# Keys and values written to DRAM once, with the loads making the doubled and shifted copies

## The chip, the cores and the metric

The kernel runs on one core of a Trainium2 chip. The metric is device time in microseconds of one execution, the median of several runs; lower is better. A core has TensorE (PE: matrix products and transposes), VectorE (DVE), ScalarE (ACT), GpSimd (POOL) and SyncE (SP, which here issues DMA transfers), each with its own list of instructions that it works through in order. Transfers are issued from SP's list and from POOL's.

## The reference, cut to what matters

One layer on a sequence of 2048 tokens with 1024 channels, all float32. Sixteen query heads share four key and value heads of 64 channels; attention reaches back over 128 positions.

```python
h = rms_norm(x, norm_g)
u = h @ w_in
v_c, b_c, c_c, z_c, q, k, v, z_a, gate_logits = split(u)
y_c = b_c * causal_depthwise_conv(c_c * v_c, conv_w) * silu(z_c)
y_a = y_c @ w_conv_out
q = rms_norm(q per head, q_norm_g); k = rms_norm(k per head, k_norm_g)
o = sliding_window_attention(q, k, v, sinks) * silu(z_a)   # banded blocks of 128
y_b = o @ w_attn_out
g_a, g_b = split(sigmoid(gate_logits + gate_b))
return x + (g_a * y_a + g_b * y_b) @ w_out
```

## The kernel before

The sequence is worked through in two tiles of T = 1024 tokens, each as two halves of H = 512. Products run at full float32 accuracy by splitting every operand into a high part and a low part (`split`): high by high, high by low and low by high. Most projections (`sunit`) form seven such products in place of eight by a Strassen-like scheme; the first tile's keys and values come from a plain unit (`cunit`).

The order of all work is written out by hand. `run` advances a counter, the tick, once for each piece of a TensorE unit, some 2.7 to 3.5 us; `put(n, f)` places a step `f` at tick `n`, and `ahead_loads` issues weight loads two units ahead, from SP. A tick therefore fixes the order of instructions in each engine's list, and the semaphores between engines fix the rest.

Temporary tiles of 2 KB a partition come from one pool of 19 buffers (`big`, through `slot`). Which buffer a tile gets is decided when the program is built, by the builder's reckoning of which falls free first; the first write to a tile then waits for the last use of the tile that had the buffer before.

Per tile of tokens the order is: keys, values, four units of queries, then the convolution's units (`cv`, `b`), gates (`ga`, `gb`), the two gated branches (`za`, `z`), and the branch outputs (`ya`, `yb`). The last stage, `o`, is for the whole sequence.

Keys, queries and values go to DRAM scratch tensors and come back in the arrangement that the attention wants:

- `fin_q` (L605) writes a normalised query's high and low part to `q2d`, four writes for each 512 tokens of a unit, from POOL.
- `fin_k` (`back`, L672) writes a key unit's high and low part to `kd`, one write for each of two heads and each part, from POOL. A head's 64 channels are written twice, to partitions 0 to 63 and 64 to 127.
- `fin_v` (L699) writes values, token on the partitions, to `vd[block, partition, kind, head, high and low]`. There are four kinds for each block: the block itself (kind 1), the block shifted by 64 tokens (kind 0), and each of its and its predecessor's halves doubled over both halves of the partitions (kinds 2 and 3). Each pair of blocks takes seven writes, from POOL. `zero_prev` fills the part of the first block that has no predecessor.

`attention` places, for each of 8 blocks of 128 tokens and 4 key heads of a tile, seven steps: `att_load` at tick n - 4 (from SP: queries L714, keys L719 or L721 and L723, values L725), `att_scores` at n (L738: eight products of a query tile as stationary operand with 192 key columns as moving operand), `att_exp`, `att_norm`, `att_turn` (transposes, then four selections on POOL, L792), `att_values` at n + 7 (L809) and `att_out` (from SP, L822). The values tile `v2` is the stationary operand of `att_values`.

## Time and profile before

| | |
|---|---|
| runs | 2031.86, 2033.07, 2033.2 us; median 2033.07 |
| the profiled execution: its own time | 2032.55 us |
| its span, first to last instruction | 2030.8 us |
| granted TensorE clock, mean | 0.999 |
| busy: TensorE, DVE, ACT, POOL | 2002.3, 1385.3, 936.9, 429.2 us |
| DMA | 329.15 MB, mean 162 GB/s |
| writes of values and keys, from POOL | 112 and 32, median 0.61 us to issue |
| landing of those writes, median | 3.6 to 4.0 and 5.4 to 6.0 us |
| loads of queries, keys and values, from SP | 64, 68 and 64; landing 3.6 to 4.4 us |

The rows are read from the profile of one execution. A busy row adds up the time of an engine's instructions, without those that issue transfers; the times of those come from the groups by line. "Waited for" names the event that ended an engine's idle time, with the total, the number of times and the longest. A row of the timeline gives the start, the duration, the engine, the line, the operation, output and input, and in square brackets the idle time just before it with what ended it. Clock 1.00 is full speed.

### The profile page before, as it was taken

Reading aid. Unit: us, or ns where it says so; the run is one execution under the profiler, and the core shown is the slowest. Engines: PE = TensorE matmul, PEld = TensorE weight load, DVE = VectorE, ACT = ScalarE, POOL = GpSimd, SP = SyncE. Lnnn points to the kernel's source line nnn. Section 1 sums busy time; section 2 is a strip of 40 time slices with the busy share of each in tenths; the row PEclk is TensorE's granted clock in tenths of the full one; section 3 lists DMA queues with packets and bytes.
Section 4 is the critical chain, followed back from the end, with each engine's and each line's share of the span. In section 5 each row is a group of like instructions: output and inputs, shape, how many; then the busy total and the mean of one; then the engine's idle time right before and its main releaser. Section 6 shows DMA issues by size and latency. Waiting matters only on the chain.

```text
span 2030.8 us, 27523 instructions
## 1 busy us (share of the span) xinstructions
PE 2002.3 (99%) x9488; PEld 1664.3 (82%) x9488; DVE 1385.3 (68%) x2360; ACT 936.9 (46%) x1847; POOL 429.2 (21%) x597
## 2 busy tenths in 40 slices
PE   8999999999999999999999999999999999999999
PEld 6787888888888887888878888888888887888887
DVE  6877787787675555348768887787776656356654
ACT  6554455456664333244545544455665334212321
POOL 1873222222321000000277222222332000100000
PEclk9999999999999999999999999999999999999999
DMA  6794424445555534664498434445555443765553
GB/s 177 223 241 137 131 83 122 133 131 173 156 173 164 176 110 148 230 221 154 126 255 215 128 100 138 128 122 168 162 177 173 148 146 129 249 214 167 174 171 109
DMA packets 339594, 329.15 MB, mean 162 GB/s; under 512 B 21804, under 2 KB 260448, under 8 KB 339456
## 3 DMA queue, kind: packets, MB, share of 16 engines
q1 hardware_dynamic: 321984, 276.37, 43.9%
q0 software_dynamic: 17456, 51.04, 9.2%
q8 instruction: 75, 1.23, 0.2%
q14 instruction: 63, 0.52, 0.1%
q10 hardware_dynamic: 16, 0.00, 0.0%
HBM read 217.61 MB, written 109.71 MB: 161 GB/s over the span
## 4 chain that ended last, share of the span: by engine, by line
PE 71%; DVE 4%; ACT 3%; issue 3%; DMA 1%; POOL 1%; SPq 0%; POOLq 0%; DVEq 0%; ACTq 0%
PE Y L364 21%; PE yb L938 9%; PE ya L938 8%; PE Vcv L364 2%; PE Xcv L364 2%; PE Xza L364 2%; PE Vz L364 2%; PE Vo L364 2%; PE Xo L364 2%; PE Xz L364 2%; PE Vza L364 2%; PE s L738 2%; PE Xgb L364 2%; PE po L809 1%; PE Xga L364 1%
## 5 line engine op out<-in xcount | busy, mean ns | idle before, releaser
L792 POOL TENSOR_SCALAR_AFFINE_SELECT xh<-xh 64x512 fp32r<-64x512 f32 x64 | 69.4, 1085 | 644.7 <-DVE xl L784 477.6
L763 ACT ACTIVATE p<-s,st,rq 128x128 f32<-128x128 f32 x256 | 113.5, 453 | 0.6
L699 POOL DMA_DIRECT2D vd<-v x112 | 69.4, 626 | 197.3 <-DVE v L207 186.4
L210 DVE TENSOR_TENSOR o<-po,o 64x256 f32<-64x256 f32 x128 | 53.7, 420 | 67.4 <-ACT o L820 61.2
L971 DVE SCALAR_TENSOR_TENSOR tha<-tha,ya 128x512 f32<-128x512 f32 x32 | 22.0, 687 | 100.8 <-PE ya L938 93.9
L820 ACT COPY o<-po 64x256 f32<-64x256 f32 x128 | 47.0, 367 | 83.6 <-DVE o L210 82.1
L938 PE MATMUL ya<-opa,wya_0h 128*128 128x512 f32 x256 | 79.5, 391 | 2.4 <-ACT opa L206 1.9
L364 PE MATMUL Xcv<-oph,wcv_ah 128*128 128x512 f32 x256 | 80.1, 394 | 0.0
L938 PE MATMUL yb<-opb,wyb_0h 128*128 128x512 f32 x256 | 79.4, 391 | 0.0
L938 PE MATMUL yb<-opb,wyb_1h 128*128 128x512 f32 x256 | 79.4, 391 | 0.0
L938 PE MATMUL ya<-opa,wya_1h 128*128 128x512 f32 x256 | 78.8, 389 | 0.0
L738 PEld LDWEIGHTS s<-k,q 128*128 128x128 f32 x512 | 65.6, 191 | 9.0 <-ACT p L763 5.4
L206 ACT CAST opb<-ocr 128x512 fp32r<-128x512 f32 x32 | 19.9, 621 | 111.5 <-DMA ocr<-ocd 109.8
L784 DVE TENSOR_TENSOR xl<-pt,xh 128x512 fp32r<-128x512 f32 x64 | 44.1, 690 | 39.7 <-ACT yp L783 33.9
L738 PE MATMUL s<-k,q 128*128 128x192 f32 (+2 forms) x512 | 67.2, 274 | 2.9 <-ACT p L763 2.7
L991 DVE SCALAR_TENSOR_TENSOR thb<-thb,yb 128x512 f32<-128x512 f32 x32 | 21.9, 686 | 55.2 <-PE yb L938 53.5
L938 PEld LDWEIGHTS ya<-opa,wya_0h 128*128 128x128 f32 x256 | 48.0, 188 | 13.6 <-ACT opa L206 2.8
L858 DVE SCALAR_TENSOR_TENSOR y<-u,cols,y 128x512 f32<-128x512 f32 x64 | 50.1, 784 | 10.6 <-ACT y L851 8.6
L1025 POOL DMA_DIRECT2D wo<-in_w_out x16 | 8.7, 544 | 226.1 <-DVE opb L207 209.7
L938 PEld LDWEIGHTS ya<-opa,wya_1h 128*128 128x128 f32 x256 | 48.1, 188 | 10.0
L792 POOL TENSOR_SCALAR_AFFINE_SELECT yp<-xl 64x512 fp32r<-64x512 f32 x64 | 55.3, 864 | 3.1
L938 PEld LDWEIGHTS yb<-opb,wyb_1h 128*128 128x128 f32 x256 | 47.6, 188 | 9.6
(583 smaller groups left out, 6246.3 us busy)
## 6 DMA issues: line engine op xcount, KB each, us to landing
wcv_raw<-in_w_in SPq DMA_DIRECT2D x64, 256.0 KB, 4.6
q<-q2d SPq DMA_DIRECT2D x64, 256.0 KB, 3.7
v<-vd SPq DMA_DIRECT2D x64, 256.0 KB, 4.4
gd<-th SPq DMA_DIRECT2D x64, 256.0 KB, 2.2
k<-kd SPq DMA_DIRECT2D x56, 256.0 KB, 4.4
vd<-v POOLq DMA_DIRECT2D x96, 128.0 KB, 3.6
wq_raw<-in_w_in SPq DMA_DIRECT2D x32, 256.0 KB, 4.3
q2d<-q_h POOLq DMA_DIRECT2D x64, 128.0 KB, 4.9
```

Source lines behind the costliest of these rows:

```text
L210: return (eng or nc.vector).tensor_tensor(out=o, in0=a, in1=b, op=ALU.add)
L364: nc.tensor.matmul(ps, lhsT=w[:, j, :], rhs=b[:, m, :], start=start and j == 0 and i == 0, stop=j == KP - 1 and i == 2, skip_group_check=n ...
L699: nc.gpsimd.dma_start(to.rearrange("b p h d -> p b h d"), v[half].bitcast(F32).rearrange("p b e l d -> p b e (l d)"))
L738: nc.tensor.matmul(sp[:, h, c, skip : 3 * HD], lhsT=q2[:, h, c, :], rhs=k2[:, l, h * HD + skip : h * HD + 3 * HD], start=l == 0, stop=l == 1)
L763: nc.scalar.activation(out=p[:, i, :], in_=sg[:, i, HD : 3 * HD], func=AF.Exp, bias=st[:, 1, i : i + 1], scale=rv[:, i // 2, i % 2 : i % 2 ...
L784: nc.vector.tensor_tensor(out=xl, in0=pt, in1=xh.bitcast(F32), op=ALU.subtract)
L792: nc.gpsimd.affine_select(out=d4, in_=s4, pattern=[[0, 2 * G], [-sg, HD]], compare_op=ALU.is_gt if prev else ALU.is_ge, fill=0.0, base=0, ...
L820: nc.scalar.copy(ov, pov[oth, :, :, e, :])
L858: nc.vector.scalar_tensor_tensor(out=y, in0=u[:, h * H + i : h * H + i + H], scalar=tap(i, k), in1=y, op0=ALU.mult, op1=ALU.add)
L938: nc.tensor.matmul(ps, lhsT=w[:, j, cs], rhs=o[:, m, :], start=p == 0 and j == 0 and i == 0, stop=p == 1 and j == KP - 1 and i == 2)
L971: nc.vector.scalar_tensor_tensor(out=m, in0=m, scalar=1.0, in1=ps, op0=ALU.add, op1=ALU.mult)
L991: nc.vector.scalar_tensor_tensor(out=m, in0=m, scalar=1.0, in1=ps, op0=ALU.add, op1=ALU.mult)
```

## The change

Keys and values are written once, and the loads make the copies.

- `kd[t]` becomes `[head, channel, half block of 64 tokens, high or low, 64]`. `back` issues two writes for each call, one for each part, with both heads in one write; a partition's 512 tokens go out as eight runs of 64. The load reads the 64 channels twice, into both halves of the partitions (`twice`), and the tile `k2` is now ordered by half block and then part, so that the moving operand of the scores is three pieces of 64 columns.
- `vd` becomes `[token + 128, head, high and low]`. One call of `fin_v` issues two writes in place of fourteen, one for each pair of blocks. `att_load` issues four value loads in place of one: the two full arrangements (kinds 0 and 1), each of 128 tokens, and the doubled halves, once into each half of the partitions.
- `zero_prev` is one write in place of three.

The order of TensorE, DVE and ACT instructions is the same in both programs. SP has 192 more transfers to issue, POOL 114 fewer.

```diff
-    kd = [dram.tile([NKV, P, 2, T], F32, name=f"kd{t}") for t in range(NT)]
-    vd = dram.tile([S // P + 1, P, 4, NKV, P], F32, name="vd")
+    kd = [dram.tile([NKV, HD, 2 * NB, 2, HD], F32, name=f"kd{t}") for t in range(NT)]
+    vd = dram.tile([S + P, NKV, P], F32, name="vd")
...
     def zero_prev():
-        nc.gpsimd.dma_start(vd[0, LH, 0], zv[LH])
-        for n in (2, 3):
-            nc.gpsimd.dma_start(vd[0, :, n], zv)
+        nc.gpsimd.dma_start(vd[0:P].rearrange("p h d -> p (h d)"), zf)
...
             split(hi, lo, pt)
-            for e in range(2):
-                for l, src in enumerate((hi, lo)):
-                    nc.gpsimd.dma_start(
-                        kd[t][2 * i + e, :, l, hs(q)].rearrange("(o d) t -> d o t", d=HD),
-                        src[HALVES[e]].bitcast(F32).unsqueeze(1).to_broadcast([HD, 2, H]))
+            for l, src in enumerate((hi, lo)):
+                nc.gpsimd.dma_start(
+                    kd[t][2 * i : 2 * i + 2, :, q * 2 * HB : (q + 1) * 2 * HB, l].rearrange(
+                        "o d b x -> (o d) b x"),
+                    src.bitcast(F32).rearrange("p (b x) -> p b x", x=HD))
...
-                    b0 = t * NB + q * HB + 2 * bp
-                    ALL = slice(0, P)
-                    for kind, off, dst, half in (
-                            (1, 0, ALL, ALL), (0, 0, UH, LH), (0, 1, LH, UH),
-                            (2, 1, LH, LH), (2, 1, UH, LH), (3, 1, LH, UH), (3, 1, UH, UH)):
-                        to = vd[b0 + off : b0 + off + 2, dst, kind, 2 * i : 2 * i + 2, :]
-                        nc.gpsimd.dma_start(
-                            to.rearrange("b p h d -> p b h d"), v[half].bitcast(F32).rearrange("p b e l d -> p b e (l d)"))
+                    r0 = t * T + q * H + (2 * bp + 1) * P
+                    nc.gpsimd.dma_start(
+                        vd[r0 : r0 + 2 * P, 2 * i : 2 * i + 2].rearrange("(b p) h d -> p b h d", p=P),
+                        v.bitcast(F32).rearrange("p b e l d -> p b e (l d)"))
...
+    def twice(ap):
+        return ap.unsqueeze(0).to_broadcast([2] + list(ap.shape))
...
-        k2 = slot([P, 2, 2 * P], F32R, f"k2_{nm}")
+        k2 = slot([P, 4, 2, HD], F32R, f"k2_{nm}")
...
         if b > 0:
-            nc.sync.dma_start(k2.bitcast(F32), kd[t][j, :, :, (b - 1) * P : (b + 1) * P])
+            nc.sync.dma_start(
+                k2.bitcast(F32).rearrange("p b l x -> p (b l x)"),
+                twice(kd[t][j, :, 2 * b - 2 : 2 * b + 2].rearrange("d b l x -> d (b l x)")))
...
-        nc.sync.dma_start(v2.bitcast(F32), vd[gb, :, :, j, :])
+        r0 = gb * P
+        for i in range(2):
+            nc.sync.dma_start(v2[:, i].bitcast(F32), vd[r0 + (1 + i) * HD : r0 + (3 + i) * HD, j])
+        for half in HALVES:
+            nc.sync.dma_start(
+                v2[half, 2:4].bitcast(F32), vd[r0 : r0 + P, j].rearrange("(n k) d -> k n d", n=2))
...
-                        rhs=k2[:, l, h * HD + skip : h * HD + 3 * HD], start=l == 0, stop=l == 1)
+                        rhs=k2[:, h + skip // HD : h + 3, l, :], start=l == 0, stop=l == 1)
```

More of the change, by code (lines that the diff above doesn't have):

```diff
@@ L151, in block_kernel @@
     hbias = consts.tile([P, 2 * KC], F32, name="hbias")
-    zv = zf.rearrange("p (h d) -> p h d", d=P)
     def zero_prev():
-        nc.gpsimd.dma_start(vd[0, LH, 0], zv[LH])
-        for n in (2, 3):
-            nc.gpsimd.dma_start(vd[0, :, n], zv)
+        nc.gpsimd.dma_start(vd[0:P].rearrange("p h d -> p (h d)"), zf)
     def prep_gain():
@@ L716, in att_load, with keys @@
             q2d[t][j][:, 2 * b : 2 * b + 2].rearrange("p h c e x -> p (h c e x)"))
-        k2 = slot([P, 2, 2 * P], F32R, f"k2_{nm}")
+        k2 = slot([P, 4, 2, HD], F32R, f"k2_{nm}")
+        def keys(n, t, b):
+            nc.sync.dma_start(
+                k2[:, n : n + 2].bitcast(F32).rearrange("p b l x -> p (b l x)"),
+                twice(kd[t][j, :, 2 * b : 2 * b + 2].rearrange("d b l x -> d (b l x)")))
         if b > 0:
-            nc.sync.dma_start(k2.bitcast(F32), kd[t][j, :, :, (b - 1) * P : (b + 1) * P])
+            nc.sync.dma_start(
+                k2.bitcast(F32).rearrange("p b l x -> p (b l x)"),
+                twice(kd[t][j, :, 2 * b - 2 : 2 * b + 2].rearrange("d b l x -> d (b l x)")))
         else:
-            nc.sync.dma_start(k2[:, :, P:].bitcast(F32), kd[t][j, :, :, 0:P])
+            keys(2, t, 0)
             if gb > 0:
-                nc.sync.dma_start(k2[:, :, :P].bitcast(F32), kd[t - 1][j, :, :, T - P : T])
+                keys(0, t - 1, NB - 1)
         v2 = slot([P, 4, P], F32R, f"v2_{nm}")
-        nc.sync.dma_start(v2.bitcast(F32), vd[gb, :, :, j, :])
+        r0 = gb * P
+        for i in range(2):
+            nc.sync.dma_start(v2[:, i].bitcast(F32), vd[r0 + (1 + i) * HD : r0 + (3 + i) * HD, j])
+        for half in HALVES:
+            nc.sync.dma_start(
+                v2[half, 2:4].bitcast(F32), vd[r0 : r0 + P, j].rearrange("(n k) d -> k n d", n=2))
         return q2, k2, v2
```

## The prediction

> **What bounds the kernel.** I read the page's busy row and slices first, then the waits of TensorE, then the timeline round the longest of them.

> ```profile
> span 2030.8 us, 27523 instructions
> PE 2002.3 (99%) x9488; PEld 1664.3 (82%) x9488; DVE 1385.3 (68%) x2360; ACT 936.9 (46%) x1847; POOL 429.2 (21%) x597
> ...
> POOL 1873222222321000000277222222332000100000
> ```

> TensorE works through one fixed list and is idle for 28.5 us in all. The change leaves that list as it is, so it can win only from those 28.5 us (and any stretch at a lower clock), and lose by adding idle time. POOL, off the path on average, is at 7 to 8 tenths in slices 2, 3, 21 and 22: there it issues the writes of v, k and q for each tile of 1024 tokens. TensorE's own waits, longest first (total, times, longest):

> ```profile
> PE s L738 <- ACT p L763: 2.7, 4, 1.2
> PE Y L1098 <- POOL zero L129: 2.6, 1, 2.6
> PE Y L364 <- DVE Vq L210: 2.2, 1, 2.2
> PE pt L779 <- DVE p L216: 2.2, 2, 1.8
> PE ya L938 <- ACT opa L206: 1.9, 2, 1.0
> PE ptq L572 <- DVE qss L581: 1.6, 1, 1.6
> ```

> No wait is on a load. Two of these places hang on what the change touches.

> **Second tile, q units (1015 to 1068 us).** Start, duration, instruction, and in brackets the idle time before it:

> ```profile
> 1016.69 0.72 ACT L600 ACTIVATE q_h<-q_t,gqk 128x512 fp32r<-128x512 f32 x1
> 1055.59 0.71 POOL L605 DMA_DIRECT2D q2d<-q_h  x1 [0.81 <-DMA vd<-v]
> 1056.83 0.75 DVE L601 SCALAR_TENSOR_TENSOR q_l<-q_t,gqk,q_h 128x512 fp32r<-128x512 f32 x1 [7.67 <-DMA kd<-k_l]
> 1053.21 0.73 PE L364 MATMUL Y<-oph,wq_sh 128*128 128x512 f32 x2 [0.73 <-ACT Y L382]
> 1061.17 0.73 PE L364 MATMUL Y<-oph,wq_th 128*128 128x512 f32 x2 [2.20 <-DVE Vq L210]
> ```

> The first q half is ready at 1017.4 and its write is issued at 1055.6: POOL's queue is 38 us behind with v and k. Tiles not yet written out keep their buffers of the pool of 19, so DVE stands 7.7 us for one, and TensorE 0.73 + 2.20, and 0.3 more at 1067.7.

> **First attention block (166 to 194 us).**

> ```profile
> 167.34 0.59 ACT L434 COPY q_t<-Y 128x512 f32<-128x512 f32 x1 [3.52 <-PE s L738]
> 167.39 0.75 DVE L601 SCALAR_TENSOR_TENSOR q_l<-q_t,gqk,q_h 128x512 fp32r<-128x512 f32 x1 [4.42 <-PE s L738]
> 168.89 1.09 PE L572 MATMUL ptq<-ident,q_t 128*128 128x128 f32 x4 [1.59 <-DVE qss L581]
> 186.17 0.69 DVE L784 TENSOR_TENSOR xl<-pt,xh 128x512 fp32r<-128x512 f32 x1 [2.00 <-issue]
> 194.07 0.50 PE L364 MATMUL Vcv<-oph,wcv_sl 128*128 128x512 f32 x1 [1.34 <-DVE wcv_sl L270]
> ```

> In the built program, which gives each tile's address and no time, `q_t` and `q_l` of the last q unit lie in the buffers of block 0's keys and queries, and `xl` of block 0 in that of block 1's queries. So ACT and DVE wait for scores that TensorE reaches by its list, and TensorE then waits for them.

> **The change, part by part.**

> *POOL's issues.* Per tile, 56 writes of v and 16 of k become 8 and 8. Before: 48 at 0.61, 8 at 0.72 (the full-width v rows), 16 at 0.61: 44.8 us. After: v 8 at 0.72; a key write is 128 partitions of eight 256-byte runs, and its nearest row is the q write's 0.69 for 64 such partitions; ends 0.61 and 1.4, I take 0.85. Sum 12.6, so 32 us less per tile. POOL also idles for landings there (0.4 to 1.7 us each time), and 56 fewer transfers shorten that too. The last k_l is ready at 1011.9; POOL then issues it by about 1013, before the first q half. The 3.2 us of TensorE go: **-3.2** (ends 0 and -3.7, by which its products start later there than their pace). In tile 0 the same backlog costs TensorE no row of its own; I take nothing.

> *Buffers.* The planner hands out buffers by its own reckoning of when they fall free. With fewer writes, 926 of the 1065 tiles change place. In the built changed program `q_t` and `q_l` follow q tiles that are long done, and `xl` follows one too. Holding each tile's first write in the trace against the last use of its new predecessor (POOL's writes moved up as above), one wait is new: block 2's keys for block 0's `p`, 175.8 to 182.5, on SP. Behind it queue block 2's v and the next weights; scores come at 202.4, and v itself waited until 191.3 before. So 1.6 at 168.9 goes, and at 194.07, where `xl` can start 2 us sooner, 1.3: **-2.9** (ends 0 and -3.3).

> *The clock.* Two stretches, with busy times of PE, PEld, DVE, ACT and POOL, then the granted clock, DMA share and GB/s:

> ```profile
> 165.40:168.80 3.40, 1.90 (x13) 1.59 (x11) 1.41 (x3) 1.43 (x3) 0.25 (x1) 1.00 0.18 48
> 168.80:172.30 3.50, 3.41 (x10) 2.91 (x11) 3.50 (x5) 2.27 (x4) 3.50 (x6) 0.51 0.64 119
> ```

> After the stretch with TensorE busy for 1.90 of 3.40 us comes one at half clock, costing half of 3.4. Without the gap: **-1.7** (ends 0 and -1.7). [...]

> *SP.* A block's v load becomes four issues of 128 runs each; the nearest rows are 0.32 to 0.43 for 128 runs, so 1.5 against 0.55; the key load has half as many pieces. That is +1.0 a block, 64 us over both tiles, in front of SP's next entries: stores, weight loads, the next q. Weight loads are read 17 us or more after issue. After a v load SP mostly stands 1 to 15 us for a store's data, which hides it. Pushing every later issue back until the next such stand moves 8 of 64 q loads, by at most 1.3 us, each with 10 us or more in hand. **0** (ends 0 and +21, first rival). The bytes written fall by 8.4 MB a tile; DMA's share is 0.5 in these stages, so nothing.

> *Key layout.* The scores' moving rows become three pieces of 64 columns.

> ```profile
> 166.29 1.00 PE L738 MATMUL s<-k,q 128*128 128x64 f32 x8
> 401.23 1.03 PE L738 MATMUL s<-k,q 128*128 128x192 f32 x8
> ```

> Eight products of 64 and 128 columns take as long as eight of 192: the weight load sets the pace, and a short break hides under it. No row has such a layout. **0** (ends 0 and +17, second rival).

> Sum: -3.2 - 2.9 - 1.7 = -7.8. The profiled execution is 2032.55 (span 2030.8 and 1.75 round it), 0.5 under the median of 2033.07; from the median, **2025.3 us**.

> **Rivals.** A measurement of this kernel tells about 0.2% (4.1 us) from no change.

> - *SP late (slower).* Place: q and k loads with the least lead. At 1355.49 a q load goes out for scores at 1362.8; the key load follows 0.5 later and lands in 4.4 at the median, so 2.4 are left; 15 of 64 blocks have leads under 9.5, 3.6 spare on average. It decides from 3 us of delay; at 5 us they lose 15 x 1.4 = 21: 2046. For it: a q issue held 1.85 at 1361.92 by earlier transfers. Against: these 15 follow a store's wait, not a v load. 0.06.
> - *Broken key rows (slower).* 512 columns pass in 0.227 us, so 192 in 0.085; the pace of 0.111 leaves 26 ns, 13 a break. At 30 a break, 34 x 504 = 17: 2042. For it: no row. Against: the pair above. 0.05.
> - *Late key writes.* The runs of a key write shrink from 2 KB to 256 bytes and could land late. Rows: q writes of 256-byte runs land in 4.7 to 4.9 us, k writes of 2-KB runs in 5.4 to 6.0, so no penalty is seen. [...] With eight in flight, 16 writes pace POOL as before only from 44.8 x 8 / 16 = 22 us each; then the 3.2 stay: 2028.5. 0.05.
> - *One place only is mended.* DVE, busy 75.6 of the 105 us from 995 to 1100, stays late by itself: 2028.5; or the first block's stall returns by another buffer: 2029.9. 0.15, half each.
> - *Nothing moves*: the writes were hidden anyway and other buffers bind: 2033. 0.07.

> The forecast has 0.62.

> **The numbers.** Faster by over 0.2% (under 2029.0): 0.62 + 0.05 + 0.07 = 0.74. Same: 0.08 + 0.07 = 0.15. Slower 0.11. Range: down to 2022.5, as the ends of the two waits give 0.9 more and the runs before spread by 1.3; up to 2030.5, past both halves of the partial case. That leaves out 0.07 + 0.11 and little else.

> **What would show it.** Right: POOL's first q write of tile 1 within some us of its data; no `Y <- Vq` or `ptq <- qss` wait; no half clock at 168.8; scores at 0.11 a product; v in four issues near 0.38. Wrong: TensorE waits on `k` or `v` loads, scores over 0.12 a product, key writes landing after 20 us, or fresh waits of ACT or DVE on buffers.

## The result, and the profile after

The changed kernel takes 2043.29 us (median of 6 runs, 2039.83 to 2045.7), the kernel before 2032.22 (6 runs beside it): a ratio of 1.0053, 95% interval 1.0042 to 1.0065, so 11 us slower where 8 us faster was forecast.

The head of the profile after, and TensorE's waits in the whole span (total, times, longest):

```profile
span 2041.3 us, 27651 instructions
PE 2007.0 (98%) x9488; PEld 1665.9 (82%) x9488; DVE 1385.4 (68%) x2360; ACT 936.7 (46%) x1847; POOL 363.5 (18%) x483
...
POOL 1353222222220000000253222222232000100000
```

```profile
PE s L750 <- DMA k<-kd: 11.4, 12, 1.9
PE Y L1110 <- POOL zero L131: 2.6, 1, 2.6
PE s L750 <- DMA wb_raw<-in_w_in: 2.1, 1, 2.1
```

POOL's slices 2, 3, 21 and 22 fell from 7 and 8 tenths to 5 or less, as forecast. (POOL's busy row does count the instructions that issue its transfers, other than the note under the first table says: its 597 became 483, which are the 114 writes fewer.) Two of the waits shown before, `Y <- Vq` (2.2) and `ptq <- qss` (1.6), are gone. In their place the scores wait for key loads, 11.4 us in twelve waits; the wait put down to `wb_raw` is one more of them, at a block whose key load had gone out 9.4 us earlier. In the profile before, TensorE waited for no load.

POOL's queue at the second tile's q units, the first q half's high part and the first write of it:

```profile
1017.02 0.72 ACT L598 ACTIVATE q_h<-q_t,gqk 128x512 fp32r<-128x512 f32 x1
1019.49 0.70 POOL L603 DMA_DIRECT2D q2d<-q_h  x1 [0.21 <-issue]
```

It is 2 us behind, not 38. Both programs give TensorE the same 9488 products in the same order, so the starts can be subtracted pair by pair. The changed kernel gains 5.0 us between 150 and 200 us and 4.1 at the second tile's q units, the two places of the forecast, and loses 19.8 elsewhere, nearly all of it in waits right ahead of scores and in three stretches at half clock; the sum is +10.7. Such a loss, with the key load's issue (SP), the scores that wait for it (PE), and two windows of 3.41 us, the one that holds the wait and the next (columns as in the windows of the prediction):

```profile
579.97 0.53 SPq L721 DMA_DIRECT2D k<-kd  x1
589.64 1.11 PE L750 MATMUL s<-k,q 128*128 128x192 f32 x8 [1.93 <-DMA k<-kd]
```

```profile
587.90:591.31 3.41, 1.67 (x11) 1.57 (x12) 2.55 (x4) 1.07 (x2) 0.99 (x1) 1.00 0.44 118
591.31:594.72 3.41, 3.41 (x10) 2.64 (x9) 1.73 (x5) 0.00 (x0) 0.00 (x0) 0.50 0.74 211
```

The keys went out 7.7 us before TensorE was ready for them and came 1.9 too late; then TensorE ran a window at half clock. Where scores wait, they start 8.3 to 9.7 us after the key load's issue. In the kernel before, scores started as little as 6.8 after the issue without waiting for keys, and key loads landed in 4.4 at the median (number, KB of each, median us to landing):

```profile
k<-kd SPq DMA_DIRECT2D x56, 256.0 KB, 4.4
```

### The profile page after: what moved, and what is told of

Same layout as the page of the kernel before. It is cut to its first block, busy times and chain, and to the rows that moved or that the text cites. A ratio compares the mean times of both kernels' runs of the same rounds, so it can differ in the third digit from the quotient of the medians.

```text
span 2041.3 us, 27651 instructions
## 1 busy us (share of the span) xinstructions
PE 2007.0 (98%) x9488; PEld 1665.9 (82%) x9488; DVE 1385.4 (68%) x2360; ACT 936.7 (46%) x1847; POOL 363.5 (18%) x483
## 4 chain that ended last, share of the span: by engine, by line
PE 70%; DVE 9%; issue 7%; DMA 5%; ACT 3%; POOL 2%; SPq 1%; POOLq 0%; DVEq 0%; ACTq 0%
PE Y L362 21%; PE yb L950 9%; PE ya L950 8%; DMA k<-kd 4%; PE Xcv L362 3%; PE Vcv L362 3%; PE Xza L362 2%; PE Vz L362 2%; PE Vo L362 2%; PE Xo L362 2%; PE Xz L362 2%; PE Vza L362 2%; PE Vq L362 2%; PE Xq L362 2%; PE s L750 2%
## 5 line engine op out<-in xcount | busy, mean ns | idle before, releaser
L750 PE MATMUL s<-k,q 128*128 128x192 f32 (+2 forms) x512 | 69.0, 277 | 15.4 <-DMA k<-kd 11.4
L794 ACT CAST xh<-pt 128x512 fp32r<-128x512 f32 x64 | 37.4, 585 | 40.3 <-PE pt L791 39.5
L362 PEld LDWEIGHTS Xcv<-oph,wcv_ah 128*128 128x128 f32 x256 | 48.1, 194 | 9.4
L950 PEld LDWEIGHTS yb<-opb,wyb_0h 128*128 128x128 f32 x256 | 47.6, 188 | 9.6
```

Source lines behind the costliest of these rows:

```text
L362: nc.tensor.matmul(ps, lhsT=w[:, j, :], rhs=b[:, m, :], start=start and j == 0 and i == 0, stop=j == KP - 1 and i == 2, skip_group_check=n ...
L750: nc.tensor.matmul(sp[:, h, c, skip : 3 * HD], lhsT=q2[:, h, c, :], rhs=k2[:, h + skip // HD : h + 3, l, :], start=l == 0, stop=l == 1)
L794: nc.scalar.copy(xh, pt)
L950: nc.tensor.matmul(ps, lhsT=w[:, j, cs], rhs=o[:, m, :], start=p == 0 and j == 0 and i == 0, stop=p == 1 and j == KP - 1 and i == 2)
```

## The theories and the experiments

Theory 1: the doubled load reads a source whose outermost dimension is 2 (`twice` puts the copies in front of the 64 channels), so it is spread over 2 of the 16 DMA engines. For it, before any run: the packet counts. Each of the kernel before's 1052 SP transfers left 16 small completion packets in queue 1 (4 bytes, 16832 in all); of the changed kernel's 1244 transfers, 952 such packets are missing (18952 are there), which is 14 for each of the 68 key loads and leaves 2. A key load is 128 runs of 2 KB at 84 ns each (the median of those packets): by these, an estimate, 64 x 84 ns = 5.4 us on two engines and 0.7 on sixteen. That an outermost dimension of 2 gives two engines is so far the theory; the packets alone show the 2. Rivals: SP issues too much (theory 2), or reading rows twice, or the new layout in DRAM, is slow in itself (theory 3).

### Two key loads, one for each half of the partitions

```diff
-                twice(kd[t][j, :, 2 * b - 2 : 2 * b + 2]...)
+            for half in HALVES:
+                nc.sync.dma_start(k2[half]..., kd[t][j, :, 2 * b - 2 : 2 * b + 2]...)
```

Expected: 

> The changed kernel with each block's key load made as two loads, one for each half of the partitions, 64 rows each; one issue more a block. Theory 1 (the doubled load, whose source has an outermost dimension of 2, runs on 2 of the 16 DMA engines and lands about 9 us after its issue, where 4.4 did before; TensorE then waits for keys): the loads are spread over 16 engines again and land in 4 to 5 us, TensorE waits on no key load, the time is 2022 to 2026. Theory 2 (SP issues too much and is late): with 0.3 to 0.5 us more of issue in a block the waits on key loads stay or grow, 2043 to 2060. Theory 3 (the same DRAM rows read twice, or the new key layout in DRAM, are slow in themselves): as changed, 2040 to 2046.

Measured: 2025.05 us against 2031.36 of the kernel before, 0.9965 (0.9953 to 0.9978). No wait on a key load is left, and the load lands in less than half the time (KB of each, median us to landing):

```profile
k<-kd SPq DMA_DIRECT2D x112, 128.0 KB, 3.9
```

Theory 1 holds and the others fall: one more issue a block, the same rows read twice and the same layout, and yet 18 us less than the changed kernel.

### The other way round: the kernel before with a source of 2 x 64 rows

```diff
-  nc.sync.dma_start(k2.bitcast(F32), kd[t][j, :, :, (b - 1) * P : (b + 1) * P])
+  nc.sync.dma_start(k2.bitcast(F32), twice(kd[t][j, 0:HD, :, (b - 1) * P : (b + 1) * P]))
```

Expected: 

> The kernel before, its DRAM layout and issues kept; only the key load reads its first 64 rows twice (the second 64 hold the same numbers), so that its source has an outermost dimension of 2. Theory 1: key loads land in 8.5 to 9.5 us, TensorE gets waits on key loads that the kernel before lacks, and the time rises by 12 to 25 us, to 2044 to 2057. Theory 2: the issues are the same, so no change, 2030 to 2034. Theory 3 in its part on layout: no change; in its part on rows read twice: slower as in theory 1.

Measured: 2075.9 us, 1.0217 (1.0203 to 1.0231). The fault alone costs 44 us in the kernel before; the direction is theory 1's, the size is well beyond its 12 to 25. The group of the scores' products (busy, mean ns, and behind the second bar the idle time ahead of them), here and then in the kernel before:

```profile
L742 PE MATMUL s<-k,q 128*128 128x192 f32 (+2 forms) x512 | 70.6, 281 | 33.6 <-DMA k<-kd 27.4
```

```profile
L738 PE MATMUL s<-k,q 128*128 128x192 f32 (+2 forms) x512 | 67.2, 274 | 2.9 <-ACT p L763 2.7
```

That is 31 us more of idle time, and ten windows at half clock in place of one, 9 x 1.7 = 15; a few us come back elsewhere. In its waits the scores start 9.3 to 11.1 us after the key load's first issue, and 13.7 at one block (the second tile's first); the median is 9.9, and 9.0 in the changed kernel. About half of that difference is, by an estimate from the packets' medians (46 ns for 1 KB, 84 for 2 KB), the load's 256 runs of 1 KB, 128 x 46 ns = 5.9 us on an engine in place of 5.4. The issues did not stay the same in one respect: the value load behind the key load held SP for 3.0 us at the median, in the kernel before for 0.55. Why, and how much of the 44 us it makes, is open. The estimate had counted neither this nor the half clock.

The number of packets in queue 1 (then MB, and the share of 16 engines), here and in the kernel before, differs by the same 952:

```profile
q1 hardware_dynamic: 321032, 276.36, 43.4%
```

```profile
q1 hardware_dynamic: 321984, 276.37, 43.9%
```

### As many engines as copies: the dose

The changed kernel, its key load reading 8 rows sixteen times, or 32 rows four times, in place of 64 rows twice; bytes, issues and buffers stay, and wrong keys reach the scores.

```diff
-        return ap.unsqueeze(0).to_broadcast([2] + list(ap.shape))
+        return ap[0 : P // 16].unsqueeze(0).to_broadcast([16, P // 16] + list(ap.shape[1:]))
```

Expected of sixteen: 

> The changed kernel, its key load reading the first 8 of the 64 rows sixteen times (outermost dimension 16) in place of 64 rows twice: same bytes, same issues, same buffers; wrong keys reach the scores, only its time is read. Theory 1: 16 engines, landing 4 to 5 us, 2022 to 2026. Theories 2 and 3 (issues; rows read more than once): 2040 to 2050, waits on key loads as in the changed kernel.

Expected of four: 

> The changed kernel, its key load reading 32 rows four times (outermost dimension 4) in place of 64 rows twice; wrong keys reach the scores, only its time is read. Theory 1: 4 engines, each with 32 runs of 2 KB at 84 ns, 2.7 us in place of 5.4 on two and 0.7 on sixteen; landing 6 to 7 us after the issue, with 7.2 as the least lead: few or no waits, 2022 to 2028. If the rows read again are slow, or a fixed cost of a doubled source is what delays it: 2038 to 2046.

Measured: sixteen 2024.31 us, 0.9960 (0.9948 to 0.9973); four 2026.62, 0.9977 (0.9968 to 0.9986). Queue 1 (packets, MB, share of 16 engines) with two, four and sixteen copies:

```profile
q1 hardware_dynamic: 315400, 276.38, 43.9%
```

```profile
q1 hardware_dynamic: 315536, 276.38, 44.4%
```

```profile
q1 hardware_dynamic: 316352, 276.38, 45.1%
```

Against sixteen copies, two lack 952 packets, 68 x 14, and four lack 816, 68 x 12: read as one for each engine, the completion packets count 2, 4 and 16 engines. With two loads a block there are 317440 packets, 68 x 16 more than with sixteen copies: all sixteen engines for each load. With sixteen the load lands in 4.7 us at the median and no score waits for it; the block shown above got its keys without a wait 7.6 us after the issue. With four, TensorE stands idle ahead of three scores for 1.4 us in all, 0.7 at most. Reading rows again cost nothing by itself: 2024.31 us with 8 rows read sixteen times, 2025.05 with 64 rows in each of two loads. The starts of the products in the changed kernel, taken against this run of sixteen copies, differ by +18.3 us: that is the price of the two engines. Idle time ahead of scores (15.4 against 2.7) is 12.7 of it, and two more windows at half clock (three against one) are 3.4; I have not placed the other 2.2.

### Values alone, keys alone

The kernel before with one half of the change each (for the keys, with the load in two).

Expected of the values alone: 

> The kernel before with the change to the values alone: 8 writes of values a tile in place of 56, four value loads a block in place of one; key writes and key load as before. Theory 1: no wait on key loads, and at least the gain of the shorter POOL queue at the second tile's q units (3 to 4 us); the 5 us in the first block hang on which buffers the planner picks, so 2022 to 2030. Theory 2 (the three added issues a block are what costs): 2038 to 2046, with waits of TensorE on q, k or v loads.

Expected of the keys alone: 

> The kernel before with the change to the keys alone (8 key writes a tile in place of 16, two key loads a block by halves, three pieces of 64 columns in the scores); values as before. POOL's queue shrinks by some 3 of its 38 us, so by the prediction's cause the second tile's q units gain 0 to 1 and the first block loses its two waits, by another place of the buffers: 2025 to 2029, no wait on key loads, products of the scores at 0.11 us. If the key writes alone were what held POOL, both gains come: 2022 to 2025. If the key layout or the two loads cost something: over 2031.

Measured: values alone 2024.34 us, 0.9962 (0.9949 to 0.9974), no wait on keys or values; the three more issues a block cost nothing. Keys alone 2026.36, 0.9975 (0.9966 to 0.9984), so layout and writes cost nothing either; a product of the scores takes 274 ns in both, as before. Against the expectation, the profile of keys alone has one wait on a key load, 2.3 us at the second tile's first block, with a window at half clock behind it. The q units of the second tile lost their waits too (4.1 us), which I had expected only of the values. POOL is still 29 us behind there.

### Eight key loads a block: SP late, by itself

Expected: 

> The changed kernel with a block's key load made as eight loads of 16 partitions each, seven more issues a block, about 2.5 us more of SP's time in front of the values and of the next entries: the prediction's rival of a late SP, by itself. By that rival's own point (it decides from 3 us of delay): the last piece goes out 2.5 us later, of the least lead of 7.2 some 4.7 are left, a landing takes 4 to 5: 0 to 5 us lost against two loads, 2024 to 2030. If SP's issues are the scarcer thing: 2032 to 2050 with waits on q, k or weights.

Measured: 2024.51 us, 0.9967 (0.9955 to 0.9980), and TensorE waits for no load. The eight issues take 3.6 to 6.4 us at a block (two took 1.1), and still the time is that of two loads (2025.05). The rival of a late SP is not what happened, and it is further away than I had put it.

### POOL's backlog, put back in two doses

The kernel with two key loads, and beside each value write six or nine more writes from POOL to a scratch tensor.

```diff
+                    for n in range(6):   # the other run: 9
+                        half = HALVES[n % 2]
+                        nc.gpsimd.dma_start(vx[n, r0 : r0 + 2 * P, ...][half], v[half]...)
```

Expected of six: 

> The changed kernel with two key loads a block, and POOL's backlog put back: beside each value write, six more writes of half its partitions to a scratch tensor that nothing reads (48 a tile, as many as the change took away). In the built program q_t and xl of the first attention block still follow tiles that are long done. If the two gains have the two causes of the prediction, the waits at 168 and 194 us stay away (-5 against the kernel before, half clock included) and the waits of TensorE at the second tile's q units (Vq, Y at 1050 to 1070 us) come back: 2025.5 to 2029. If POOL's queue is not the cause of those waits, they stay away and the time is 2022 to 2025.

Expected of nine: 

> As the run with six extra value writes, with nine in their place (72 a tile): POOL's backlog is about 15 us longer than with six and about as long as in the kernel before (38 us) or longer. In the built program the planner now gives the first block's q_t, q_l and xl the same predecessors as in the kernel before (block 0's keys and queries, block 1's queries), which with six it did not. If the two gains have the two causes of the prediction, both are gone: waits of TensorE of about 1.6 and 1.3 us at 166 to 194 us, and of 2 to 4 us at the second tile's q units, 2029 to 2034 in all. If the gain at 166 to 194 us comes from elsewhere than the buffers, those waits stay away; if the one at the q units comes from elsewhere than POOL's queue, those stay away: 2024 to 2028 with either.

Measured: six 2025.23 us, 0.9971 (0.9959 to 0.9982); nine 2038.88, 1.0036 (1.0022 to 1.0050). With six, POOL's first q write comes 29 us after its data, and none of the waits returned: a miss. With nine it comes 42 us late, and they did, at both places (after the total, the times and the longest):

```profile
PE Y L363 <- ACT Y L381: 2.8, 1, 2.8
...
PE ptq L571 <- DVE qss L580: 1.6, 1, 1.6
```

The second is the wait of the first block; in the built program its tiles have the predecessors of before again, and with six they had not. Nine came out over the expected 2029 to 2034: TensorE loses 3.1 us more at the q units than in the kernel before, waits 2.3 for keys at the second tile's first block, and has three windows at half clock.

Buffers and backlog both changed between six and nine. The second profile of the kernel before (next section) tells them apart: its buffers are those of before and the first block waits, its backlog is 33 us and the q units do not. So the planner's buffers decide the first block's wait, and POOL's backlog the one at the q units, from a point between 33 and 38 us. The extra writes put back bytes as well as issues, so which of the two makes the backlog matter is not shown. Below that point the backlog comes out later: with six, the first block's query and key loads of the second tile go out at 1083.5, where the changed kernel has them at 1070.8, and the scores wait.

```profile
1083.53 0.34 SPq L716 DMA_DIRECT2D q<-q2d  x1
1093.87 1.11 PE L758 MATMUL s<-k,q 128*128 128x192 f32 x8 [1.84 <-DMA k<-kd]
```

### Both kernels once more

Expected of the kernel before: 

> The kernel before once more, for a second profile. If the half clock follows from how much of a 3.41 us window of a free grid TensorE idles, its place depends on where the grid lies in this execution: the wait of 1.6 us at 168 us, or the one of 1.8 us at 578 or 1404 us, may or may not be followed by one; if it belongs to the first block as such, it comes at 168 again. 2030 to 2034.

Expected of the changed kernel: 

> The changed kernel once more, for a second profile: the waits on key loads at the same places and of the same size (11 to 14 us in all); by the grid of windows the half clock follows other waits than at 591, 1233 and 1301 us, and any that covers over 1.6 us of one window. 2039 to 2046.

Measured: 2030.04 and 2045.23 us. In the second execution of the kernel before, POOL's first q write came 33 us after its data and not 38, and TensorE did not wait at the q units:

```profile
1015.05 0.72 ACT L600 ACTIVATE q_h<-q_t,gqk 128x512 fp32r<-128x512 f32 x1
1049.11 0.71 POOL L605 DMA_DIRECT2D q2d<-q_h  x1
```

It waited 1.5 for block 0's keys at 1096.9 in their place. The wait at 168 us was there (1.59) without a half clock; that came at 1405.7, after another wait. The changed kernel again waited for key loads, 14.9 us in fourteen waits, a little over the 11 to 14 expected. Two of its three stretches at half clock followed the same waits as in the first profile (now at 590 and 1235 us), where I had expected other ones.

## Why the prediction was wrong, point by point

**The key load, put at 0, is the step that failed.** It stands in the part on SP: "the key load has half as many pieces", and in the first rival, where the key load "lands in 4.4 at the median". I took the landing from the row of before, because bytes were the same and pieces fewer, and asked only what the issue costs. The issue did stay (0.53 us against 0.52). What changed is how many engines share the pieces, by the packets 2 in place of 16: 8.3 to 9.7 us from issue to scores in the blocks that wait, and +18.3 us by the dose. The shape of the new source, 2 x 64 x 512, stood in the diff; the row of before said nothing of such a shape, and this is where the bounds should have been wide, from 0.7 to 5.4 us of transfer by the packets' 84 ns.

**The rival with the right place.** "SP late" named the blocks with little lead and priced 5 us of delay at +21; +18.3 came, with ten of the thirteen late scores at the 15 blocks it had counted. That the two numbers are so near is partly luck: the rival had 21 us of idle time and no half clock, the runs 12.7 and 3.4. Its cause was wrong: SP's issues were not late, even eight key loads a block cost nothing. I gave 0.06 to a delay of keys from one cause, and nothing to a late landing.

**POOL's queue, -3.2.** The wait went (-3.7 by the three intervals, -4.1 with what follows), and nine more writes brought it back. But it was not in every execution of the kernel before, as its second profile shows: a backlog of 38 us makes TensorE wait there, one of 29 or 33 leaves 1.5 to 2.3 us at block 0's keys. One profile's row was priced as if every execution had it.

**Buffers, -2.9.** Right in cause and size: -1.75 at the first of the two waits and -1.50 at the second, with and without the faulty load, and back when the old predecessors were.

**The clock, -1.7.** The window at 168 us went, but the term was no property of that place (last section): the changed kernel has three others.

**SP, 0, and the key layout, 0.** Both right in effect. The four value issues take 2.3 us and not 1.5, and nothing waited for it. Key writes of 256-byte runs land in 4.1 to 5.7 us, no later than before. One reading there was wrong: the writes that fall away lie where DMA's share was 0.80 (45 to 150 us) and 0.89 (995 to 1100), not 0.5. It is 0.56 and 0.72 in the changed kernel, and no run shows what that alone is worth.

With the load mended or one half of the change left out, five versions of the change came out between 2024.3 and 2026.4 (0.9960 to 0.9975), which is 5.6 to 7.4 below the kernel before beside them: the sum of -7.8 was the worth of the rest of the change, a little too high. Of the versions with all of the computation, values alone (2024.34) and the whole change with two or eight key loads (2025.05, 2024.51) beat both kernels and can't be told apart.

## What to carry to other kernels

When a load makes copies, look at the outermost dimension of its source before counting bytes or pieces: here two copies in front left 2 completion packets a load in place of 16, and four and sixteen copies left 4 and 16; two transfers of 64 rows, at one more issue, had 16 each again and landed in 3.9 us. A landing time may be taken over from the old kernel only for the same shape; for a new one, estimate it by pieces per engine times the packet's duration (here 64 x 84 ns = 5.4 us, where sixteen engines give 0.7), and hold it against the lead of each consumer (6.8 us at the least here). And a wait that one profile shows needs a second profile before it is priced.

## What the runs showed of the hardware

```profile
1229.61:1233.02 3.41, 1.33 (x11) 1.30 (x11) 0.87 (x2) 0.00 (x0) 0.54 (x1) 1.00 0.52 147
1233.02:1236.43 3.41, 3.41 (x10) 2.63 (x9) 2.61 (x6) 0.00 (x0) 0.00 (x0) 0.50 0.90 267
1413.93:1417.34 3.41, 1.86 (x12) 1.51 (x11) 2.10 (x6) 2.16 (x5) 0.70 (x2) 1.00 0.44 153
1417.34:1420.75 3.41, 3.41 (x22) 3.02 (x23) 2.42 (x4) 2.39 (x4) 0.71 (x2) 1.00 0.85 235
```

Two pairs of neighbouring windows of the changed kernel: 1.33 us busy, then half clock (0.50); 1.86 us busy, 55%, and the clock stays at 1.00.
